# Softmax-weighted values on one core: two heads copied in pairs of row blocks, one check of all values, a skipped loop that counts semaphores in registers

## The chip, the core and the metric

One core of a Trainium2 chip runs the whole program. Its engines are TensorE (PE, with a separate row PEld for weight loads), VectorE (DVE), ScalarE (ACT), GpSimd (POOL) and SyncE (SP); 16 DMA engines move data between DRAM and the on-chip memory SBUF. TensorE writes its results to a second memory, PSUM; the kernel's tiles there take a bank each, 2 KB in each of 128 partitions. The metric is the device time of one execution in microseconds, the median over runs. A profiled execution gives a span, from the first to the last recorded instruction, and its own time, which is a little longer.

## What is computed

```python
def reference(scores, v):            # scores 8 x 12 x 1024 x 1024, v 8 x 12 x 1024 x 64, fp32
    scores_max = np.max(scores, axis=-1, keepdims=True)
    attn = np.exp(scores - scores_max)
    attn = attn / (np.sum(attn, axis=-1, keepdims=True) + 1e-8)
    return np.matmul(attn, v).astype(np.float32)
```

There are 96 heads. For each, the rows of a 1024 x 1024 matrix of scores are turned into weights that sum to one, and these are multiplied with 1024 values of 64 numbers.

## The kernel before

The kernel does not subtract the row maximum. It takes exp(scores) in fp16, appends a column of ones to v, so that one product gives the weighted values and the sum of the weights, and divides. This is right only where sums and values lie in a safe range. The kernel therefore gathers the reciprocal of every row's sum and the largest value of v, tests both, and at the end has a number (`count`) of partitions that passed. If it is less than 128, a second, general loop computes everything again with the maximum subtracted (`general`, line 330); with these inputs it is skipped by a jump (line 469).

The main loop (line 461) runs 24 times over groups of four heads (k = 0 to 3). A head's scores lie as eight row blocks of 128 rows (r = 0 to 7), in one of four buffers `s_nat` of 4 MB. In a head:

- ScalarE takes the exponential of two row blocks at a time (line 414, 128x2048), or of one in the group's last head, into one of eight buffers `p_nat`.
- TensorE turns each block's eight 128x128 pieces (line 427) into a PSUM tile `psT`. There are four, of one block each.
- VectorE copies each `psT` to SBUF, into one of four `pt` (line 434, 128x1024 fp16).
- TensorE multiplies `pt` with `vones`, the values with their ones, eight products into a PSUM bank `psO` (line 173, in `finish`). Four row blocks share a bank, so a head has two banks, and there are two sets. Products follow the turned blocks three row blocks later (`LAG`).
- After the fourth and the eighth block VectorE inverts the sums of the bank into `seen` (`invert`, line 150) and multiplies (`normalise`, line 158, two instructions), into `out_sb`.
- GpSimd converts the values of a head four ahead into `vones` (`spread_v`, line 270, four copies a head).

VectorE also reduces each of the four `vones` to its largest absolute value, twice in head 0 and twice in head 1 (`watch_v`, line 287), and tests these in head 2 (`spread_of`, lines 281 and 282, and `within`, lines 300 and 308). At the group's end `judge` does the same with `seen`, and a product with ones gives `count` (lines 304, 308, 324, 328).

SyncE issues all transfers on one queue, in an order written out by hand (`queue`, `load` at 249, `load_v` at 261, `store` at 194): loads as soon as ScalarE has read a buffer, one store of two heads after head 1 and one after head 3. Each engine's order is a scheduler's, except where `after` or `in_line` fix it: TensorE's whole order, each reduce of `vones` behind a copy, and the last reciprocal of a first bank ahead of the last copy. The main loop lets semaphores count on across iterations and waits against registers (`iteration_sync="reg_based"`); the general loop resets its semaphores in each iteration.

Behind the loop all engines pass a barrier, load `count` into a register (line 468, where SyncE also tests that it lies between 0 and 128), jump over the general loop, and meet in two closing barriers (listed under line 496, the launch). In a barrier each engine reports with a DRAIN and GpSimd releases all.

## Time and profile before

| | |
|---|---|
| median of 3 runs | 1068.48 us (1068.08 to 1069.45) |
| time of the profiled execution | 1067.78 us |
| its span | 1066.0 us |
| mean granted TensorE clock | 0.825 |
| busy: PE, DVE, ACT, POOL | 727.3, 786.2, 741.1, 244.8 us |
| HBM read, written | 436.21 MB, 25.17 MB |

In the profile's groups of instructions a row is a source line with its engine, operation, tiles and count, then its busy time and the mean of one, then the time its engine sat idle before it and what ended that. A row with a small q behind the engine's name is the engine's sequencer (jumps, semaphores, drains, DMA issues), which is not counted as busy. The table by stage gives each engine's busy time in a stretch of the span. Instruction queues in the DMA part carry the engines' own code.

```profile
L434 DVE COPY pt<-psT 128x1024 f16<-128x1024 f16 x768 | 513.9, 687 | 189.1 <-PE L173 77.3
L158 DVE TENSOR_TENSOR out_sb<-psO,seen 64x256 f32<-64x256 f32 x380 | 160.2, 422 | 63.6 <-DMA out_dram<-out_sb 52.4
```

Over the whole span VectorE's largest row is the 768 copies, one for each row block of each head, 687 ns in the mean.

### The profile page before, as it was taken

How to read it: one execution, taken by the hardware profiler on the slowest of the kernel's cores; microseconds unless marked ns; L12 is line 12 of the kernel's file. 1: busy time of each engine (PE TensorE's matmuls, PEld its weight loads, DVE VectorE, ACT ScalarE, POOL GpSimd, SP SyncE). 2: the span in 40 equal slices, each digit the busy share in tenths (PEclk: the TensorE clock that was granted, in tenths of full speed). 3: DMA queues.
4: the chain of work that ended last, by engine and by line, in shares of the span. 5: the costliest groups of instructions: out<-in, count | busy, mean ns of one | idle time of the engine just before them, and what ended most of it. 6: DMA issues, size and time to landing. Idle time of an engine off the chain costs nothing.

```text
span 1066.0 us, 33658 instructions
## 1 busy us (share of the span) xinstructions
PE 727.3 (68%) x12312; PEld 692.9 (65%) x12312; DVE 786.2 (74%) x1660; ACT 741.1 (70%) x484; POOL 244.8 (23%) x406
## 2 busy tenths in 40 slices
PE   2766866677766667676676766767766667666775
PEld 2766756666766667666675766667765667666674
DVE  1876867868678677776777777868677677786786
ACT  3756776666867668586676776666767668586685
POOL 3113212131121311212113211131121311212113
PEclk9888888878788888887888888878788787887888
DMA  9999999999999999999999999999999999999995
GB/s 393 431 423 434 424 438 430 432 432 428 432 433 433 429 436 433 433 433 432 434 427 439 433 433 433 431 435 432 433 432 433 422 440 433 432 432 427 434 427 206
DMA packets 25014, 453.08 MB, mean 425 GB/s; under 512 B 2800, under 2 KB 2800, under 8 KB 9392
## 3 DMA queue, kind: packets, MB, share of 16 engines
q1 hardware_dynamic: 25008, 453.00, 99.1%
q8 instruction: 4, 0.07, 0.0%
q14 instruction: 2, 0.02, 0.0%
HBM read 436.21 MB, written 25.17 MB: 433 GB/s over the span
## 4 chain that ended last, share of the span: by engine, by line
DMA 61%; PE 11%; PEld 8%; ACT 5%; DVE 5%; issue 4%; POOL 2%; SPq 1%; POOLq 1%; ACTq 0%; DVEq 0%
DMA s_nat<-in_scores_dram 61%; PE psT L427 6%; ACT p_nat L414 5%; PE psO L173 5%; PEld L427 5%; DVE pt L434 5%; PEld L173 4%; POOL vones L270 2%; SPq L261 1%; SPq L249 0%; POOLq L270 0%; POOLq L385 0%; POOLq L461 0%; POOLq L389 0%; DVE out_sb L158 0%
## 5 line engine op out<-in xcount | busy, mean ns | idle before, releaser
L414 ACT ACTIVATE p_nat<-s_nat 128x2048 f16<-128x2048 f32 (+1 forms) x456 | 709.4, 1630 | 219.0 <-DMA s_nat<-in_scores_dram 173.2
L427 PE MATMUL psT<-order,p_nat 128*128 128x128 f16 x6144 | 570.3, 251 | 227.5 <-ACT p_nat L414 216.3
L434 DVE COPY pt<-psT 128x1024 f16<-128x1024 f16 x768 | 513.9, 687 | 189.1 <-PE L173 77.3
L427 PEld LDWEIGHTS <-p_nat 128*128 128x128 f16 x6144 | 461.3, 125 | 244.8 <-ACT p_nat L414 232.6
L270 POOL CAST vones<-v_sb 32x512 f16<-32x512 f32 x400 | 244.1, 610 | 814.1 <-PE L427 385.0
L173 PE MATMUL psO<-vones,pt 128*128 128x65 f16 x6144 | 358.5, 205 | 34.6 <-DVE pt L434 33.0
L173 PEld LDWEIGHTS <-pt 128*128 128x128 f16 x6144 | 301.2, 106 | 48.7 <-DVE pt L434 42.6
L158 DVE TENSOR_TENSOR out_sb<-psO,seen 64x256 f32<-64x256 f32 x380 | 160.2, 422 | 63.6 <-DMA out_dram<-out_sb 52.4
L414 ACT ACT_TABLE_LOAD x24 | 30.8, 1283 | 94.1 <-PE psO L173 52.8
L287 DVE TENSOR_REDUCE v_seen<-vones 128x1 f32<-128x512 f16 x96 | 65.1, 679 | 0.8
L324 PE MATMUL psO<-vones,right 128*1 128x1 f16 x24 | 3.9, 164 | 69.2 <-DVE right L308 69.2
L324 PEld LDWEIGHTS <-right 128*1 128x1 f16 x24 | 1.9, 79 | 72.2 <-DVE right L308 72.2
L150 DVE RECIPROCAL seen<-psO 128x4 f32<-128x4 f32 x192 | 33.7, 176 | 8.6 <-PE psO L173 8.6
L308 DVE SCALAR_TENSOR_TENSOR right<-seen,part 128x1 f16<-128x1 f32 x24 | 10.5, 437 | 0.8
L308 DVE SCALAR_TENSOR_TENSOR fits<-v_seen,part 128x1 f32<-128x1 f32 x24 | 10.0, 415 | 0.0
L328 DVE CAST count<-psO 1x1 int32<-1x1 f32 x24 | 3.5, 146 | 6.2 <-PE psO L324 6.2
L304 DVE SCALAR_TENSOR_TENSOR part<-seen,fits 128x1 f32<-128x1 f32 x24 | 4.6, 192 | 0.8
L281 DVE TENSOR_REDUCE seen<-seen 128x1 f32<-128x33 f32 x24 | 4.5, 187 | 0.8
L281 DVE TENSOR_REDUCE v_seen<-v_seen 128x1 f32<-128x5 f32 x24 | 3.8, 159 | 0.7
L282 DVE TENSOR_REDUCE seen<-seen 128x1 f32<-128x33 f32 x24 | 4.2, 177 | 0.0
L282 DVE TENSOR_REDUCE v_seen<-v_seen 128x1 f32<-128x5 f32 x24 | 3.6, 149 | 0.0
L300 DVE TENSOR_SCALAR part<-v_seen 128x1 f32<-128x1 f32 x24 | 3.5, 144 | 0.0
(12 smaller groups left out, 2.8 us busy)
## 6 DMA issues: line engine op xcount, KB each, us to landing
s_nat<-in_scores_dram SPq DMA_DIRECT2D x96, 4096.0 KB, 32.3
v_sb<-in_v_dram SPq DMA_DIRECT2D x24, 1024.0 KB, 18.5
out_dram<-out_sb SPq DMA_DIRECT2D x47, 512.0 KB, 26.2
s_nat<-in_scores_dram SPq DMA_DIRECT2D x2, 2048.0 KB, 31.3
s_nat<-in_scores_dram SPq DMA_DIRECT2D x1, 1536.0 KB, 32.2
s_nat<-in_scores_dram SPq DMA_DIRECT2D x3, 512.0 KB, 20.7
s_nat<-in_scores_dram SPq DMA_DIRECT2D x1, 1024.0 KB, 25.1
out_dram<-out_sb SPq DMA_DIRECT2D x1, 256.0 KB, 3.0
```

The lines of the kernel that those rows point to most:

```text
L150: return nc.vector.reciprocal(out=recip, in_=psO[:, :, D : D + 1])
L158: nc.vector.tensor_tensor(out=st["out_sb"][h * W : (h + 1) * W, t, b * G : (b + 1) * G, :], in0=psO[part, :, 0:D], in1=recip[part].to_broa ...
L173: product = nc.tensor.matmul(out=bank[:, g * M : (g + 1) * M], lhsT=pt[:, c * P : (c + 1) * P], rhs=st["vones"][:, c, 0:M], start=(c == 0) ...
L261: nc.sync.dma_start(out=v_sb[:].rearrange("x h s l d -> x (h s l d)"), in_=rows[bass.ds(n // AHEAD, 1)].rearrange("o x y -> (o x) y"),)
L270: spread = nc.gpsimd.tensor_copy(out=vones_bufs[k][s * Q : (s + 1) * Q, :, 0:D].rearrange("i (h l) d -> i h l d", l=L), in_=v_sb[k * Q : ( ...
L281: nc.vector.tensor_reduce(out=tile[:, 0:1], in_=tile[:, 0 : n + 1], axis=X, op=ALU.min)
L282: nc.vector.tensor_reduce(out=tile[:, n + 1 : n + 2], in_=tile[:, 1 : n + 2], axis=X, op=ALU.max)
L287: watch = nc.vector.tensor_reduce(out=v_seen[:, 1 + k : 2 + k], in_=vones_bufs[k][:, :, 0:D], axis=mybir.AxisListType.XY, op=ALU.max, appl ...
L308: nc.vector.scalar_tensor_tensor(out=out, in0=tile[:, 0:1], scalar=low, in1=part, op0=ALU.is_ge, op1=ALU.mult)
L414: exp = nc.scalar.activation(out=p_nat[:, g : g + rows, :].rearrange("p r (x v) -> p x r v", v=Q * L), in_=s_bufs[k][:, r + g : r + g + ro ...
L427: turned = nc.tensor.transpose(out=psT[:, c * P : (c + 1) * P], in_=p_row[:, c // L, c % L, :], identity=order16[:],)
L434: copy = nc.vector.tensor_copy(out=pt[:], in_=psT[:])
```

## The change

Six things are changed.

1. `psT` and `pt` become two tiles of two row blocks each. In heads 0 and 1 VectorE copies a pair with one instruction of 128x2048; in heads 2 and 3 it copies row block by row block as before.
2. The two `psO` banks of a head become one tile. Head 0 is inverted and normalised once, after its eighth block, with one reciprocal of 128x8 and two multiplications of 64x512; the other heads as before.
3. The four `vones` become one tile. One reduce in head 0, after its sixth row block, finds the largest absolute value of all four heads, and two small instructions test it against both bounds into `fits`, which GpSimd sets to one ahead of the loop.
4. `judge` contains the test of the sums directly.
5. `values_load` no longer tests the range of `count` while running.
6. The general loop counts semaphores in registers, and some of its VectorE work goes to ScalarE and GpSimd. It is still skipped.

```diff
...
-    vones_bufs = []
-    for k in range(AHEAD):
-        vo = const_pool.tile([P, C, D + 2], FP16, name=f"vones{k}")
-        nc.vector.memset(vo[:, :, D : D + 2], 1.0)
...
+    vones = const_pool.tile([P, AHEAD, C, D + 2], FP16, name="vones")
+    nc.vector.memset(vones[:, :, :, D : D + 2], 1.0)
...
-    pt_bufs = buffers(sb_pool, 4, [P, SK], FP16, "pt")
+    pt_bufs = buffers(sb_pool, 2, [P, EB, SK], FP16, "pt")
...
-    psT_bufs = buffers(ps_pool, 4, [P, SK], FP16, "psT")
...
-    psO_bufs = buffers(ps_pool, 2 * (R // G), [P, 512], FP32, "psO")
+    psT_bufs = buffers(ps_pool, 2, [P, EB, SK], FP16, "psT")
...
+    psO_bufs = buffers(ps_pool, 2, [P, R // G, 512], FP32, "psO")
...
-    def sums(k, st, b):
-
-        psO = st["psO"][b][:, 0 : G * M].rearrange("p (g m) -> p g m", m=M)
+    def sums(k, st, *banks):
+
+        b, n = banks[0], len(banks)
+        psO = st["psO"][:, b : b + n, 0 : G * M].rearrange("p b (g m) -> p b g m", m=M)
         at = 1 + k * R + b * G
-        recip = seen[:, at : at + G].rearrange("p (g o) -> p g o", o=1)
+        recip = seen[:, at : at + n * G].rearrange("p (b g o) -> p b g o", b=n, o=1)
         return psO, recip
 
...
+    def invert(k, st, *banks):
+        psO, recip = sums(k, st, *banks)
+        return nc.vector.reciprocal(out=recip, in_=psO[:, :, :, D : D + 1])
+
+    def normalise(k, st, *banks):
+
+        psO, recip = sums(k, st, *banks)
+        b, n, h = banks[0], len(banks), k % T
         for t in range(T):
             part = slice(t * W, (t + 1) * W)
             nc.vector.tensor_tensor(
-                out=st["out_sb"][h * W : (h + 1) * W, t, b * G : (b + 1) * G, :],
-                in0=psO[part, :, 0:D],
-                in1=recip[part].to_broadcast([W, G, D]),
+                out=st["out_sb"][h * W : (h + 1) * W, t, b * G : (b + n) * G, :].rearrange(
+                    "x (b g) d -> x b g d", b=n
+                ),
+                in0=psO[part, :, :, 0:D],
+                in1=recip[part].to_broadcast([W, n, G, D]),
                 op=mybir.AluOpType.mult,
...
-        bank = st["psO"][b]
         for c in range(C):
             product = nc.tensor.matmul(
-                out=bank[:, g * M : (g + 1) * M],
+                out=st["psO"][:, b, g * M : (g + 1) * M],
...
-                rhs=st["vones"][:, c, 0:M],
+                rhs=vones[:, k, c, 0:M],
                 start=(c == 0),
...
-        if g == G - 1 and k < AHEAD - 1:
+        if k == 0 and r == R - 1:
+            invert(k, st, 0, 1)
+            normalise(k, st, 0, 1)
+        if 0 < k < AHEAD - 1 and g == G - 1:
             invert(k, st, b)
             normalise(k, st, b)
...
-    def spread_of(tile, n):
-
-        nc.vector.tensor_reduce(out=tile[:, 0:1], in_=tile[:, 0 : n + 1], axis=X, op=ALU.min)
-        nc.vector.tensor_reduce(
-            out=tile[:, n + 1 : n + 2], in_=tile[:, 1 : n + 2], axis=X, op=ALU.max
-        )
-
-    def watch_v(k, behind):
+    def watch_v(behind):
+
         watch = nc.vector.tensor_reduce(
-            out=v_seen[:, 1 + k : 2 + k],
-            in_=vones_bufs[k][:, :, 0:D],
-            axis=mybir.AxisListType.XY,
+            out=most,
+            in_=vones[:, :, :, 0:D],
+            axis=mybir.AxisListType.XYZ,
             op=ALU.max,
             apply_absolute_value=True,
         )
         after(watch, behind)
         watches.append(watch)
-
-    def within(out, tile, n, low, high, also=None):
-        part = small("part")
-        if also is None:
-            nc.vector.tensor_scalar(
-                out=part, in0=tile[:, n + 1 : n + 2], scalar1=high, scalar2=None, op0=ALU.is_le
-            )
-        else:
+        for bound, op in ((V_MIN, ALU.is_ge), (V_MAX, ALU.is_le)):
             nc.vector.scalar_tensor_tensor(
-                out=part, in0=tile[:, n + 1 : n + 2], scalar=high, in1=also,
-                op0=ALU.is_le, op1=ALU.mult,
-            )
-        nc.vector.scalar_tensor_tensor(
-            out=out, in0=tile[:, 0:1], scalar=low, in1=part, op0=ALU.is_ge, op1=ALU.mult
-        )
+                out=fits, in0=most, scalar=bound, in1=fits, op0=op, op1=ALU.mult
+            )
...
     count = small_pool.tile([1, 1], I32, name="count")
-    fits, right = small("fits"), small("right", FP16)
+    most, fits, right = small("most"), small("fits"), small("right", FP16)
+    nc.gpsimd.memset(fits, 1.0)
 
     def judge(bank):
 
-        within(right, seen, AHEAD * R, 1.0 / SUM_MAX, 1.0, also=fits[:])
-        cell = bank[0:1, G * M : G * M + 1]
+        n = AHEAD * R
+        part = small("part")
+        nc.vector.tensor_reduce(out=seen[:, 0:1], in_=seen[:, 0 : n + 1], axis=X, op=ALU.min)
+        nc.vector.tensor_reduce(
+            out=seen[:, n + 1 : n + 2], in_=seen[:, 1 : n + 2], axis=X, op=ALU.max
+        )
+        nc.vector.scalar_tensor_tensor(
+            out=part, in0=seen[:, n + 1 : n + 2], scalar=1.0, in1=fits, op0=ALU.is_le, op1=ALU.mult
+        )
+        nc.vector.scalar_tensor_tensor(
+            out=right, in0=seen[:, 0:1], scalar=1.0 / SUM_MAX, in1=part, op0=ALU.is_ge, op1=ALU.mult
+        )
+        cell = bank[0:1, 1, G * M : G * M + 1]
         in_line(
             nc.tensor.matmul(
-                out=cell, lhsT=right[:], rhs=vones_bufs[0][:, 0, D : D + 1], start=True, stop=True
...
-        nc.vector.memset(s_bufs[0][:, 3, 0 : C * M], 1.0)
+        nc.gpsimd.memset(s_bufs[0][:, 3, 0 : C * M], 1.0)
         half = SK // 2
-        with tc.For_i(0, BH * R, 1) as n:
+        with tc.For_i(0, BH * R, 1, iteration_sync="reg_based") as n:
...
             for h in range(2):
-                nc.vector.tensor_copy(out=pt[:, h * half : (h + 1) * half], in_=psO_bufs[h][:, 0:half])
+                nc.scalar.copy(out=pt[:, h * half : (h + 1) * half], in_=psO_bufs[0][:, h, 0:half])
...
-            nc.vector.tensor_scalar(
-                out=out_row, in0=psO_bufs[2][:, 0:D], scalar1=den[:], scalar2=None, op0=ALU.mult
-            )
+            nc.scalar.mul(out_row, psO_bufs[1][:, 0, 0:D], den[:])
...
-            st = dict(vones=vones_bufs[k], psO=[take(psO_bufs) for b in range(R // G)])
+            st = dict(psO=take(psO_bufs))
...
-                psT = take(psT_bufs)
+                if r % EB == 0:
+                    psT2, pt2 = take(psT_bufs), take(pt_bufs)
+                psT, pt = psT2[:, r % EB, :], pt2[:, r % EB, :]
                 for c in range(C):
                     turned = nc.tensor.transpose(
                         out=psT[:, c * P : (c + 1) * P],
                         identity=order16[:],
                     )
                     in_line(turned)
-                pt = take(pt_bufs)
-                copy = nc.vector.tensor_copy(out=pt[:], in_=psT[:])
-                rewrite(pt, copy)
-                if k < AHEAD // 2 and r in (G - 1, R - 2):
-                    watch_v(2 * k + (r > G), copy)
-                if k == AHEAD // 2 and r == 1:
-                    spread_of(v_seen, AHEAD)
-                    within(fits, v_seen, AHEAD, V_MIN, V_MAX)
+                if k < 2 and r % EB == EB - 1:
+                    copy = nc.vector.tensor_copy(out=pt2[:], in_=psT2[:])
+                    rewrite(pt2, copy)
+                if k >= 2:
+                    copy = nc.vector.tensor_copy(out=pt, in_=psT)
+                    rewrite(pt2, copy)
+                if k == 0 and r == R - 3:
+                    watch_v(copy)
                 if k == AHEAD - 1 and r == R - 1:
                     after(copy, invert(k, st, 0))
                 if r == R - 1:
...
-        spread_of(seen, AHEAD * R)
-        judge(st["psO"][-1])
+        judge(st["psO"])
...
-    good = nc.values_load(count[:], min_val=0, max_val=P)
+    good = nc.values_load(
+        count[:], min_val=0, max_val=P,
+        skip_runtime_bounds_check_because="a count of partitions, which is compared and no address",
+    )
     with tc.If(good < P, preferred_fallthrough_block=False):
```

More of the change, by code (lines that the diff above doesn't have):

```diff
@@ L215, in end @@
         for g in range(G):
-            nc.scalar.mul(done[:, g * D : (g + 1) * D], psO[:, g, 0:D], recip[:, g, :])
+            nc.scalar.mul(done[:, g * D : (g + 1) * D], psO[:, 0, g, 0:D], recip[:, 0, g, :])
         invert(k, st, 1)
@@ L219, in end @@
         nc.vector.tensor_tensor(
-            out=done[:, G * D :].rearrange("p (g d) -> p g d", d=D),
-            in0=psO[:, :, 0:D],
-            in1=recip.to_broadcast([P, G, D]),
+            out=done[:, G * D :].rearrange("p (b g d) -> p b g d", b=1, d=D),
+            in0=psO[:, :, :, 0:D],
+            in1=recip.to_broadcast([P, 1, G, D]),
             op=ALU.mult,
@@ L270, in spread_v @@
             spread = nc.gpsimd.tensor_copy(
-                out=vones_bufs[k][s * Q : (s + 1) * Q, :, 0:D].rearrange(
+                out=vones[s * Q : (s + 1) * Q, k, :, 0:D].rearrange(
                     "i (h l) d -> i h l d", l=L
@@ L316 @@
     count = small_pool.tile([1, 1], I32, name="count")
-    fits, right = small("fits"), small("right", FP16)
+    most, fits, right = small("most"), small("fits"), small("right", FP16)
+    nc.gpsimd.memset(fits, 1.0)
     def judge(bank):
-        within(right, seen, AHEAD * R, 1.0 / SUM_MAX, 1.0, also=fits[:])
-        cell = bank[0:1, G * M : G * M + 1]
+        n = AHEAD * R
[7 more added lines that the diff above has]
+        )
+        nc.vector.scalar_tensor_tensor(
+            out=right, in0=seen[:, 0:1], scalar=1.0 / SUM_MAX, in1=part, op0=ALU.is_ge, op1=ALU.mult
+        )
+        cell = bank[0:1, 1, G * M : G * M + 1]
         in_line(
             nc.tensor.matmul(
-                out=cell, lhsT=right[:], rhs=vones_bufs[0][:, 0, D : D + 1], start=True, stop=True
+                out=cell, lhsT=right[:], rhs=vones[:, 0, 0, D : D + 1], start=True, stop=True
             )
@@ L350, in general @@
                 nc.tensor.transpose(
-                    out=psO_bufs[c * P // half][:, at : at + P],
+                    out=psO_bufs[0][:, c * P // half, at : at + P],
                     in_=p_row[:, c * P : (c + 1) * P],
```

16 lines of the change are left out of this document (3 added, 13 removed).

## The prediction

> **What bounds the kernel now.** I read the page's first parts, then the stages at the end, because the page says at once where nothing can be won.
>
> ```profile
> span 1066.0 us, 33658 instructions
> ...
> DMA  9999999999999999999999999999999999999995
> ...
> q1 hardware_dynamic: 25008, 453.00, 99.1%
> ```
>
> The DMA engines are full in every slice but the last. 453 MB at some 433 GB/s are 1047 us, and no edit here changes a byte of it. So for the first 1049 us only the stream counts. The view of two whole groups of four heads (43.7 us each, 500 to 587.4 us) agrees: DMA share 1.00 in both, while VectorE is busy for 32.9 and 33.4 of 43.7 us. VectorE has about 10 us to spare per group, and what it saves there is worth nothing. What can count is after the stream, so I cut the end into stages (busy us and count by engine, then clock, DMA share, GB/s):
>
> ```profile
> core 0: us, PE busy (x) PEld busy (x) DVE busy (x) ACT busy (x) POOL busy (x), PEclk, DMA share, GB/s
> 1028.00:1035.00 7.00, 5.90 (x128) 5.66 (x126) 6.62 (x13) 5.92 (x4) 0.00 (x0) 0.99 1.01 431
> 1035.00:1042.00 7.00, 6.35 (x128) 5.71 (x126) 6.75 (x14) 6.97 (x5) 0.84 (x2) 1.00 1.00 426
> 1042.00:1049.00 7.00, 5.74 (x122) 5.33 (x120) 6.81 (x18) 6.13 (x5) 4.04 (x7) 1.00 1.01 420
> 1049.00:1056.00 7.00, 5.92 (x115) 4.99 (x112) 6.46 (x14) 5.14 (x9) 2.44 (x4) 1.00 0.48 163
> 1056.00:1061.00 5.00, 0.27 (x5) 0.08 (x1) 1.58 (x7) 0.09 (x1) 2.46 (x4) 0.78 0.24 52
> 1061.00:1066.00 5.00, 0.00 (x0) 0.00 (x0) 0.00 (x0) 0.00 (x0) 0.00 (x0) 0.50 0.02 7
> ```
>
> Two things stand here. From 1028 to 1056 VectorE is nearly full: in the last group it is the bound beside the stream. And in the last 5 us no engine works at all. VectorE's groups from 1028.6 to 1055.7 (count, busy us, mean ns, idle before):
>
> ```profile
> L434 DVE COPY pt<-psT 128x1024 f16<-128x1024 f16 x29 | 18.8, 681 | 0.7 <-PE L173 0.4
> L158 DVE TENSOR_TENSOR out_sb<-psO,seen 64x256 f32<-64x256 f32 x12 | 5.1, 421 | 0.3
> L287 DVE TENSOR_REDUCE v_seen<-vones 128x1 f32<-128x512 f16 x4 | 2.7, 678 | 0.0
> L150 DVE RECIPROCAL seen<-psO 128x4 f32<-128x4 f32 x7 | 1.2, 174 | 0.0
> ```
>
> It waits for 1 us of 27. The idle end is resolved by lines: L469 is the jump over the general loop, L496 the two closing barriers (duration min/median/max, first and last start):
>
> ```profile
> L469 SPq COMPARE_BRANCH  x2: 46/48/49, 1061.8 to 1062.1; - x2
> ...
> L469 PEldq COMPARE_BRANCH  x2: 82/133/184, 1061.9 to 1062.4; - x2
> L469 DVEq COMPARE_BRANCH  x2: 57/59/61, 1061.9 to 1062.2; - x2
> ```
> ```profile
> L496 SPq DRAIN  x2: 7/7/7, 1063.1 to 1063.2; - x2
> ...
> L496 PEldq DRAIN  x1: 8/8/8, 1062.6 to 1062.6; - x1
> L496 DVEq DRAIN  x1: 42/42/42, 1065.2 to 1065.2; - x1
> L496 POOLq EVENT_SEMAPHORE  x1: 17/17/17, 1065.3 to 1065.3; - x1
> ```
>
> Each engine jumps and reports to the barrier with its DRAIN. PE does so at 1062.6, SyncE at 1063.2. VectorE, whose last work ended at 1058.8, jumps at 1062.15 and drains only at 1065.19: 2.98 us for nothing it could wait for. In that gap lie the only instruction transfers of the stage: 16 KB from 1063.04, 8 KB from 1063.17 (queues 8 and 14; in the DMA view q14 has 2 of them, one more at 1065.8). I read it as a jump into code that was not there yet. GpSimd's answer at 1065.27 and the end at 1066.0 hang on it.
>
> **The jump.** Counted in the built programs, VectorE has 212 instructions before and 163 after; its jump goes from number 177 to 208 before, from 137 to 159 after. SyncE jumps from 127 to 172, PE from 1111 to 1153, both farther, without a stall, so distance is not the cause; a block border between 177 and 208 of VectorE is. The loop (20 to 170) runs 24 times and no instruction transfer falls into the later 23, so all code up to 170 stays in place. The new target lies at 159, below that. I take the stall as gone. Bounds: 0 if the border is elsewhere, the whole 2.98 us if not; I take the whole, and then SyncE or PE is last.
>
> [...]
>
> **SyncE and PE behind it.** SyncE's path from its first branch (1061.8) to its DRAIN (1063.2) loses three semaphore instructions of the skipped branch (0.075 apart: 0.23), the range test of values_load (L468: 191 and 37 ns, 0.32 to the next start) and two of eight closing waits (0.06 each: 0.12). 1063.18 - 0.67 = 1062.5. PE loses one semaphore instruction (0.14): 1062.64 - 0.14 = 1062.5. Barrier at 1062.5, GpSimd 0.08 later at 1062.6 instead of 1065.27: **-2.65 us**. If the stall stays, none of this shows, since VectorE is last anyway.
>
> **VectorE in the last group.** Pitches from the timeline: three copies in a row take 1.89 us, so one follows another after 0.60.
> - Copies of heads 0 and 1: 16 x 0.60 = 9.6 go. A pair copy is not in the trace. The reduce rows give the fixed part (128x5: 0.15), so 1024 elements stream for 0.53; a pair is 2 x 0.53 + 0.15 = 1.21 busy, 1.13 in a row: 8 x 1.13 = 9.0, **-0.5**. Bounds: 1.06 (streaming alone), and 2.26 if it streams as slowly per element as the 128x512 reduce (0.53 per 512). I take 1.13; the same operation's row is nearest.
> - Value check: four reduces (0.60 each, 2.4) and four small ones (0.35) go; one reduce of 2048 (4 x 0.53 + 0.15 - 0.08 = 2.2) and two small ones (0.2) come: **-0.35**.
> - Head 0's two normalisations (0.09 + 2 x 0.45 + 0.05 each: 2.1) become one: 0.22 + 2 x 0.72 = 1.65: **-0.45**.
> - Against it: the first copy waits for two transposed blocks, not one. The blocks come 0.85 apart there (PE clock 0.50 from 1024 to 1028), so it starts at 1026.3 instead of 1025.45, and the next two pairs leave gaps of 0.5 and 0.4; twice later VectorE waits 0.3 for products that a pair copy released late: **+0.85 to +2.3**, I take 1.2.
> - From head 1 on the built order puts the two multiplications right behind the reciprocal; before, a copy stood between. Reciprocal to multiplication is 0.22 instead of 0.09, but the copy then loses its 0.11 gap: **+0.02** each, four times.
>
> Sum -1.3 + 1.3: I take **-0.1**, with +0.9 and -0.9 as ends. The gain is capped: the five last exponentials run from 1048.45 to 1053.30 as the last rows land, the last transposes need 0.7 more, so the last copy can't start before 1054.05; now it starts at 1054.96.
>
> **At nothing.** Pair copies, the late normalisation and the single reduce in the other 23 groups: VectorE has 10 us to spare. Were that gone, loads take 32 us to land while 4 MB need 9.7, so they are issued some 22 us ahead. SyncE's stores wait for VectorE only after heads 1 and 3; head 0's normalisation is still earlier than head 1's. Head 0's PSUM pair is next written by head 2. GpSimd's new memset (0.1) lies ahead of a wait for v of 4.3 us. What general() holds is skipped.
>
> **The sum.** The profiled execution took 1067.78 (span 1066.0, 1.8 around it). 1067.78 - 2.65 - 0.1 = 1065.0. The median of the runs is 1068.48, 0.7 above this execution; on that footing 1068.48 - 2.75 = **1065.7**.
>
> **Rivals.**
> [...]
> 2. Slower: a pair copy, reading two PSUM banks, streams at 1 element where the 1024 copy does two. Then 2.26 instead of 1.13, 8 times, on the full VectorE of the last group: +9.0, of which about 1.5 fills the new gaps. 1065.7 + 7.5 = 1073.2. It decides from about 1.5 us a pair (8 x 0.35 eats the 2.75). Against: type and pattern are the same.
> 3. The last group's savings count in full (0.9) and the transfer at 1065.8 goes too, shortening what lies behind the span (up to 0.5): 1064.4.
>
> **How the numbers follow.** Forecast 0.74, rival 1 0.12, rival 2 0.07, rival 3 0.07. The forecast's own range is 1064.9 to 1066.6 (-0.9 to +0.9 of the last group, mostly inside). With rivals 1 and 3 the range is 1064.4 to 1068.3; rival 2 and the edges are left out. A difference counts from 0.2%, 2.1 us, about what a measurement can tell from no change. Of the forecast 0.64 lies beyond it, 0.10 within (last group 0.6 worse or more). Faster 0.64 + 0.07 = 0.71, same 0.10 + 0.12 = 0.22, slower 0.07.
>
> **What would show it.** In the new profile: VectorE's DRAIN within 0.3 us of its jump; SyncE's or PE's DRAIN last; no 8 KB instruction transfer between jump and barrier. The idle stretch behind the last store shrinks from about 4.5 to 2 us. Pair copies of 1.2 us mean; the last copy within 0.9 us of 1054.96; DMA full to 1049. Wrong would be: a DRAIN 3 us behind its jump on any engine, pair copies beyond 1.5 us, or a slice of the stream below 9.

## The result: slower, and the profile after

The changed kernel takes 1076.22 us (1075.81 to 1077.07), the kernel before in the same runs 1068.28 us: a ratio of 1.0074, with an interval from 1.0061 to 1.0087: 0.7% slower, little but clear of noise. That is 7.9 us more where 2.75 us less was forecast. The profiled execution took 1076.2 us, with a span of 1074.4 us.

The page of the changed kernel first: its span, the DMA engines in 40 slices, and the queues.

```profile
span 1074.4 us, 32373 instructions
...
DMA  9999999999999999999999999999999999999992
...
q1 hardware_dynamic: 25008, 453.00, 98.3%
q8 instruction: 4, 0.07, 0.0%
```

The stream is as full as it was, and it ends almost at the same time: the last exponential ends at 1053.8 us, before at 1053.3. So next to nothing was lost in the loads, and nearly all in what the engines do with the last group. And the queue q14, which had carried two instruction transfers of 8 KB, is gone. The stages of the end, with the columns as before:

```profile
1028.00:1035.00 7.00, 6.91 (x104) 6.75 (x103) 4.21 (x4) 5.92 (x4) 0.00 (x0) 0.69 1.03 437
1035.00:1042.00 7.00, 4.09 (x88) 3.78 (x85) 6.42 (x9) 6.89 (x5) 0.34 (x1) 1.00 0.99 421
1042.00:1049.00 7.00, 4.27 (x88) 4.00 (x89) 5.29 (x9) 6.12 (x5) 2.08 (x4) 1.00 1.01 420
1049.00:1056.00 7.00, 4.41 (x88) 4.12 (x88) 5.81 (x12) 4.84 (x5) 2.42 (x4) 1.00 0.31 128
1056.00:1063.00 7.00, 4.62 (x98) 4.38 (x96) 4.72 (x10) 0.00 (x0) 2.42 (x4) 1.00 0.17 37
1063.00:1070.00 7.00, 2.49 (x54) 2.08 (x52) 3.35 (x11) 0.93 (x4) 2.44 (x4) 0.99 0.01 2
1070.00:1074.40 4.40, 0.00 (x0) 0.00 (x0) 0.09 (x1) 0.00 (x0) 0.00 (x0) 0.50 0.26 60
```

Before, VectorE (third column) was busy for 6.5 to 6.8 of each 7 us and TensorE (first) for about 6. From 1035 to 1063 us TensorE is now busy for 4.1 to 4.6 us and VectorE for 4.7 to 6.4, and the work ends 10 us later. Neither is full there: the two wait for each other. VectorE's groups between the first copy of the last group and the last (1027.2 to 1065.8 us; count, busy us, mean ns, idle before and who ended it) and TensorE's waits from 1024 to 1068 us (us, times, longest) say where:

```profile
L430 DVE COPY pt<-psT 128x1024 f16<-128x1024 f16 x16 | 11.0, 691 | 5.2 <-PE L168 3.5 <-PE psO L168 1.5
L427 DVE COPY pt<-psT 128x2048 f16<-128x2048 f16 x8 | 9.7, 1221 | 3.7 <-PE L420 2.2 <-PE psO L168 1.5
L152 DVE TENSOR_TENSOR out_sb<-psO,seen 64x256 f32<-64x256 f32 x8 | 3.4, 422 | 0.3
L279 DVE TENSOR_REDUCE most<-vones 128x1 f32<-128x2048 f16 x1 | 2.3, 2276 | 0.0
L152 DVE TENSOR_TENSOR out_sb<-psO,seen 64x512 f32<-64x512 f32 x2 | 1.4, 688 | 0.1
```
```profile
PE psT L420 <- DVE pt L430: 6.4, 8, 0.8
...
PE psO L168 <- DVE out_sb L152: 1.6, 2, 1.3
```

TensorE's waits before, from 1024 to 1058 us, have neither:

```profile
PE psO L173 <- DVE pt L434: 2.0, 6, 0.7
PE psT L427 <- ACT p_nat L414: 1.9, 6, 0.9
```

VectorE's instructions cost what the prediction gave them (a pair copy 1.22 us, the one reduce 2.28), but VectorE now waits 5.2 us ahead of its single copies and 3.7 ahead of its pair copies. The wait that the kernel before did not have is TensorE's: eight times, once for each pair of blocks in heads 2 and 3, a transposition waits for the copy `L430`. The timeline of one such pair (start, duration, and in brackets the idle time before) shows the round trip:

```profile
1051.22 0.69 DVE L430 COPY pt<-psT 128x1024 f16<-128x1024 f16 x1
...
1051.96 0.61 PE L420 MATMUL psT<-order,p_nat 128*128 128x128 f16 x8 [0.81 <-DVE pt L430]
...
1052.64 0.69 DVE L430 COPY pt<-psT 128x1024 f16<-128x1024 f16 x1 [0.73 <-PE L168]
1052.66 0.61 PE L420 MATMUL psT<-order,p_nat 128*128 128x128 f16 x8
...
1053.60 0.69 DVE L430 COPY pt<-psT 128x1024 f16<-128x1024 f16 x1 [0.27 <-PE psO L168]
...
1054.34 0.27 PE L420 MATMUL psT<-order,p_nat 128*128 128x128 f16 x2 [0.81 <-DVE pt L430]
```

TensorE turns an even block at 1052.66. VectorE copies it at 1053.60, and only when that copy has ended (1054.29) does TensorE start on the odd block of the same pair, at 1054.34, although that block goes to the other half of the tile. Two blocks take 2.38 us; before, VectorE alone set the pace.

The end of the program did what was forecast. The jump over the general loop (`L464`) and the DRAIN behind it (`L491`), with first and last start:

```profile
L464 DVEq COMPARE_BRANCH  x2: 57/59/61, 1073.1 to 1073.2; - x2
```
```profile
L491 SPq DRAIN  x3: 7/7/7, 1073.7 to 1074.0; - x3
...
L491 DVEq DRAIN  x2: 10/10/10, 1073.4 to 1074.0; - x2
L491 PEldq DRAIN  x2: 8/37/66, 1073.7 to 1074.0; - x2
```

VectorE's DRAIN starts 0.22 us after its last jump starts (1073.23 to 1073.45); before it was 3.04 (1062.15 to 1065.19; the 2.98 of the prediction count from the end of the jump). SyncE is last at 1073.73, as forecast, behind TensorE's DRAIN at 1073.66. From the last reciprocal (1056.88 before, 1068.09 now) to the end of the span it is 9.1 us before and 6.3 now: 2.8 us won. The last copy ends 10.1 us later (1055.6, now 1065.7), and that reciprocal comes 2.4 us behind it instead of 1.3: 10.1 + 1.1 - 2.8 = 8.4 us, the difference of the spans.

Where the 10.1 us of the last copy come from can be read from three marks: the first transposition of the last group (1024.40 before, 1027.37 now), the end of the last copy of its head 1 (1041.18, 1046.53) and that of its head 3 (1055.62, 1065.71). The group starts 3.0 us late, heads 0 and 1 take 2.4 us more, heads 2 and 3 take 4.7 us more. Of the 2.4 us, 0.9 is order alone: two multiplications of head 1 now stand ahead of its last copy (from 1044.40), and stood behind it before (from 1041.21).

### The profile page after: what moved, and what is told of

It is laid out like the page before. It is cut to its first block, busy times and chain, and to the rows that moved or that the text cites. A ratio compares the mean times of both kernels' runs of the same rounds, so it can differ in the third digit from the quotient of the medians.

```text
span 1074.4 us, 32373 instructions
## 1 busy us (share of the span) xinstructions
PE 661.3 (62%) x12312; PEld 620.5 (58%) x12312; DVE 746.5 (69%) x1272; ACT 741.1 (69%) x484; POOL 243.5 (23%) x407
## 4 chain that ended last, share of the span: by engine, by line
PEld 38%; issue 29%; PE 20%; DVE 9%; PEldq 1%; ACT 1%; DVEq 0%; ACTq 0%
PEld L420 24%; PE psT L420 14%; PEld L168 13%; PE psO L168 7%; DVE pt L427 5%; DVE pt L430 2%; ACT p_nat L405 1%; DVE out_sb L152 1%; DVE part L309 0%; DVE fits L289 0%; PEldq L453 0%; DVE right L312 0%; PEldq L376 0%; DVE seen L144 0%; PEldq L380 0%
## 5 line engine op out<-in xcount | busy, mean ns | idle before, releaser
L420 PE MATMUL psT<-order,p_nat 128*128 128x128 f16 x6144 | 507.6, 234 | 180.9 <-DVE pt L430 149.0
L420 PEld LDWEIGHTS <-p_nat 128*128 128x128 f16 x6144 | 429.9, 119 | 198.4 <-issue 172.7
L168 PE MATMUL psO<-vones,pt 128*128 128x65 f16 x6144 | 322.5, 196 | 138.0 <-DVE out_sb L152 51.1
L168 PEld LDWEIGHTS <-pt 128*128 128x128 f16 x6144 | 267.4, 100 | 158.3 <-DVE pt L427 96.0
L430 DVE COPY pt<-psT 128x1024 f16<-128x1024 f16 x384 | 264.0, 691 | 130.9 <-PE L168 78.4
L427 DVE COPY pt<-psT 128x2048 f16<-128x2048 f16 x192 | 232.0, 1221 | 103.5 <-PE L420 82.7
L152 DVE TENSOR_TENSOR out_sb<-psO,seen 64x256 f32<-64x256 f32 (+1 forms) x332 | 152.9, 460 | 50.0 <-PE psO L168 28.3
L279 DVE TENSOR_REDUCE most<-vones 128x1 f32<-128x2048 f16 x24 | 54.6, 2275 | 0.0
L144 DVE RECIPROCAL seen<-psO 128x4 f32<-128x4 f32 (+1 forms) x168 | 30.5, 181 | 29.5 <-PE psT L420 14.8
L214 ACT ACTIVATE done<-psO,seen 128x64 f32<-128x64 f32 x4 | 0.9, 314 | 13.2 <-PE psO L168 13.2
L289 DVE SCALAR_TENSOR_TENSOR fits<-most,fits 128x1 f32<-128x1 f32 x48 | 7.1, 148 | 0.0
```

The costliest lines, as they stand in the source:

```text
L144: return nc.vector.reciprocal(out=recip, in_=psO[:, :, :, D : D + 1])
L152: nc.vector.tensor_tensor(out=st["out_sb"][h * W : (h + 1) * W, t, b * G : (b + n) * G, :].rearrange("x (b g) d -> x b g d", b=n), in0=psO ...
L168: product = nc.tensor.matmul(out=st["psO"][:, b, g * M : (g + 1) * M], lhsT=pt[:, c * P : (c + 1) * P], rhs=vones[:, k, c, 0:M], start=(c ...
L279: watch = nc.vector.tensor_reduce(out=most, in_=vones[:, :, :, 0:D], axis=mybir.AxisListType.XYZ, op=ALU.max, apply_absolute_value=True,)
L289: nc.vector.scalar_tensor_tensor(out=fits, in0=most, scalar=bound, in1=fits, op0=op, op1=ALU.mult)
L420: turned = nc.tensor.transpose(out=psT[:, c * P : (c + 1) * P], in_=p_row[:, c // L, c % L, :], identity=order16[:],)
```

## The experiments

Every ratio is to the kernel before, timed anew with each set of runs (e1 to e4, e5 to e8, e9 to e12); kernels of different sets are compared by their ratios. The theories in the expectations, formed as the runs came in: **A**, the two blocks of a `psT` and a `pt` pair are one tile, and what writes one half waits for what reads the other. **B**, the pair copies themselves are slow, since they wait for two blocks. **C**, VectorE's new instructions (the long reduce, the late normalisation) hold it up. **D**, the two banks of a `psO` pair are tied together in the same way as the halves in A.

### e1 to e4: the pairs of psT and pt

e1 and e2 declare accesses to different halves independent of each other, which takes the wait away and nothing else (`apart` is the kernel's own function for this). In e1:

```diff
                     in_line(turned)
+                    if k >= 2 and r % EB == EB - 1:
+                        apart(turned, copy, "two halves of a pair")
+                        apart(copy, turned, "two halves of a pair")
```

> The changed kernel, in which the transposes into the upper half of a psT pair are declared independent of the copy out of its lower half (heads 2 and 3; the two touch different elements). Theory A: the last group ends 10.1 us late because in heads 2 and 3 a pair is one tile, so TensorE may not turn the odd block before VectorE has copied the even one, and may go on only then; the 2.4 us that two blocks take there (before: about 1.8) are this round trip. By A the copies of heads 2 and 3 lose their 4.8 us, the group before ends earlier as well, so the last group starts up to 2 us sooner, and the time falls from 1076.2 to 1068 to 1071 (the copy of an even block still waits for the products of the other half of its pt pair). Theory B: the pair copies of heads 0 and 1 and the late start are to blame: 1075 to 1076.

Measured: 1072.96 us, ratio 1.0041 (1.0027 to 1.0055). e2 adds the same for products of an odd block and the copy of the next even one into the same `pt` pair (`copies` holds that copy):

```diff
             in_line(product)
+            if r % EB == EB - 1 and copies[-1] is not None:
+                apart(product, copies[-1], "two halves of a pair")
+                apart(copies[-1], product, "two halves of a pair")
...
+                copies.append(copy if k >= 2 and r % EB == 0 else None)
```

> As the run before, and the copy into the lower half of a pt pair is also independent of the products that read its upper half. Theory A: the whole coupling of the two halves is gone, heads 2 and 3 run as in the kernel before; what is left is the later first copy of the group (1.2 by the prediction) and the gain at the jump (2.4): 1066 to 1068. Theory B (pair copies of heads 0 and 1, late start): 1074 to 1076, since nothing of these is changed. Theory C (the one reduce of 2.3 us and the late normalisation of head 0 hold VectorE up): also 1074 to 1076.

Measured: 1073.83 us, 1.0048 (1.0031 to 1.0065). e3 copies pairs in all four heads:

```diff
-                if k < 2 and r % EB == EB - 1:
+                if r % EB == EB - 1:
                     copy = nc.vector.tensor_copy(out=pt2[:], in_=psT2[:])
                     rewrite(pt2, copy)
-                if k >= 2:
-                    copy = nc.vector.tensor_copy(out=pt, in_=psT)
-                    rewrite(pt2, copy)
```

> The changed kernel with pair copies in all four heads, so that no half of a tile is ever copied alone. Theory A: no round trip between the halves is left; heads 2 and 3 cost VectorE less (1.13 a pair), the last pair waits for the last single row (exponential ends at 1053.8, transposes 0.7): last copy from about 1054.8 to 1056, and the time is 1066 to 1069. Theory B: pairs are what is slow (in heads 0 and 1 of the last group 14 blocks take 16 us), so heads 2 and 3 get no better than heads 0 and 1: 1074 or more.

Measured: 1072.51 us, 1.0039 (1.0024 to 1.0053). e4 has no pairs at all:

```diff
-    pt_bufs = buffers(sb_pool, 2, [P, EB, SK], FP16, "pt")
+    pt_bufs = buffers(sb_pool, 4, [P, SK], FP16, "pt")
...
-    psT_bufs = buffers(ps_pool, 2, [P, EB, SK], FP16, "psT")
+    psT_bufs = buffers(ps_pool, 4, [P, SK], FP16, "psT")
...
-                if r % EB == 0:
-                    psT2, pt2 = take(psT_bufs), take(pt_bufs)
-                psT, pt = psT2[:, r % EB, :], pt2[:, r % EB, :]
+                psT = take(psT_bufs)
...
-                if k < 2 and r % EB == EB - 1:
-                    copy = nc.vector.tensor_copy(out=pt2[:], in_=psT2[:])
-                    rewrite(pt2, copy)
-                if k >= 2:
-                    copy = nc.vector.tensor_copy(out=pt, in_=psT)
-                    rewrite(pt2, copy)
+                pt = take(pt_bufs)
+                copy = nc.vector.tensor_copy(out=pt[:], in_=psT[:])
+                rewrite(pt, copy)
```

> The changed kernel without its pairs: psT and pt are four tiles of one block again and every block is copied by itself; the one check of the values, head 0's single normalisation and the shorter programs stay. Theories A and B: everything that was lost hangs on the pairs, so the last copy is back at 1055 to 1056 and the gain at the jump shows: 1065 to 1066.5. Theory C (the reduce of 2.3 us and the late normalisation): 1070 or more.

Measured: 1073.48 us, 1.0048 (1.0031 to 1.0065). All four lie together, some 3 us below the changed kernel and 4 to 5 above the kernel before. All that A expected is missed, though in e1 and e2 no transposition of the last group waits for a single copy any more: that coupling is real, but not all. And e4 speaks against B: without any pair the kernel is as slow as with pairs whose halves are free. e4's time is what C expected; e5 and e8 below rule C out. Something else that all four share costs most of the rest. TensorE's waits of e4 (1024 to 1066 us) and its timeline name it:

```profile
PE psO L168 <- DVE out_sb L152: 6.5, 2, 3.6
```
```profile
1039.80 1.88 DVE L425 COPY pt<-psT 128x1024 f16<-128x1024 f16 x3
...
1041.61 0.17 DVE L144 RECIPROCAL seen<-psO 128x4 f32<-128x4 f32 x1
1041.70 0.66 DVE L425 COPY pt<-psT 128x1024 f16<-128x1024 f16 x1
1042.38 0.88 DVE L152 TENSOR_TENSOR out_sb<-psO,seen 64x256 f32<-64x256 f32 x2
1043.31 0.43 PE L168 MATMUL psO<-vones,pt 128*128 128x65 f16 x8 [3.58 <-DVE out_sb L152]
...
1044.63 0.69 DVE L425 COPY pt<-psT 128x1024 f16<-128x1024 f16 x1 [1.37 <-PE psO L168]
```

TensorE stands still for 3.58 us until VectorE has multiplied out the first bank of the head (`L152`, two instructions from 1042.38). The product that waits writes the second bank. VectorE first works off all that is queued ahead of it, and since TensorE's order is fixed, no transposition passes the waiting product; then VectorE itself runs dry for 1.37 us.

### e5 to e8: the pairs of psO

e5 is e4 with four `psO` tiles of one bank again; head 0 is then inverted and normalised bank by bank:

```diff
-    psO_bufs = buffers(ps_pool, 2, [P, R // G, 512], FP32, "psO")
+    psO_bufs = buffers(ps_pool, 2 * (R // G), [P, 1, 512], FP32, "psO")
...
-        if k == 0 and r == R - 1:
-            invert(k, st, 0, 1)
-            normalise(k, st, 0, 1)
-        if 0 < k < AHEAD - 1 and g == G - 1:
+        if k < AHEAD - 1 and g == G - 1:
...
```

> The kernel of e4 (no pairs) in which psO is four tiles of one bank again, so that head 0 is inverted and normalised bank by bank as in the kernel before. Theory D, formed after e1 to e4: a psO pair is one tile too, so in heads 1 to 3 the first product into its second bank waits until VectorE has read the first bank, and at the end ScalarE's four multiplications of the first bank wait for the last product into the second. By D the two idle times of TensorE in e4 (3.6 and 2.9 us, put down to VectorE's out_sb) go, the last copy is back at 1055 to 1056, and with the stall at the jump gone the time is 1065 to 1066.5. Theory C (the one reduce of 2.3 us holds VectorE up): 1071 to 1073.5, since the reduce stays.

Measured: 1066.26 us, 0.9980 (0.9971 to 0.9990): 0.2% faster than the kernel before, as D expected. e6 makes the same edit on the changed kernel, which keeps its pairs of `psT` and `pt`:

> The changed kernel, pairs and all, with psO as four tiles of one bank again (head 0 inverted and normalised bank by bank). What it costs against e5 is the price of the psT and pt pairs alone. Theory D: the psO part goes (about 5 of the 8 us lost), the round trip between the halves stays in heads 2 and 3 (2.4 us for two blocks in place of 2.1, 8 times) with the late start of the pairs: 1067 to 1070. If the pairs' halves were most of the loss after all: 1072 or more.

Measured: 1074.33 us, 1.0057 (1.0041 to 1.0074). D's 1067 to 1070 is missed: the pairs of `psT` and `pt` alone cost nearly as much as both couplings together, 8 us above e5. Some 1.6 of these belong to the pair copies themselves, as e8 will show. e7 turns it round: the kernel before, with a head's two banks made one tile, and no other edit but to the indices in the general loop, which is skipped:

```diff
-    psO_bufs = buffers(ps_pool, 2 * (R // G), [P, 512], FP32, "psO")
+    psO_bufs = buffers(ps_pool, 2, [P, R // G, 512], FP32, "psO")
...
-                psO=[take(psO_bufs) for b in range(R // G)])
+                psO=pair(take(psO_bufs)))
```

> The kernel before with one edit: the two psO banks of a head are one tile. All instructions of all engines are the same, head 0 is still normalised bank by bank. Theory D: each head's first product into the second bank waits for VectorE, in head 0 too, and the stall at the jump stays: 1074 to 1077. Theory C, or any theory that blames VectorE's instructions: 1068 to 1069, no change.

Measured: 1093.67 us, 1.0238 (1.0220 to 1.0255): 25 us for the shape of one tile, with the same instructions. The direction is D's; the size (1074 to 1077) was missed, for a reason that the table below shows. TensorE's waits from 500 to 587.4 us, nearly two of its groups, name the wait:

```profile
PE psO L176 <- DVE out_sb L161: 19.2, 6, 3.7
```

e8 is e2 with the two banks declared independent in heads 1 to 3. Every instruction of the changed kernel is kept:

```diff
+            if b == 1 and k > 0:
+                upper.setdefault(k, []).append(product)
+                for op in lower.get(k, []):
+                    banks_apart(product, op)
...
-        return nc.vector.reciprocal(out=recip, in_=psO[:, :, :, D : D + 1])
+        op = nc.vector.reciprocal(out=recip, in_=psO[:, :, :, D : D + 1])
+        return reads_lower(k, op) if banks == (0,) else op
...
```

Here `banks_apart` calls `apart` both ways, and `reads_lower` does so for whatever reads the first bank: the reciprocal, the two multiplications, and ScalarE's four at the end.

> The kernel of e2 (the halves of a psT and a pt pair independent) in which products into the second psO bank are declared independent of what reads the first one, in heads 1 to 3. Every instruction of the changed kernel stays, the pair copies, the one reduce and the single normalisation of head 0 too; only waits between different halves go. Theory D: with both couplings gone this is what the prediction priced: 1064.5 to 1066.5. If VectorE's own instructions are to blame: 1070 or more.

Measured: 1067.90 us, 0.9994 (0.9985 to 1.0004). This settles C as the cause of the loss, for VectorE does in it all that it does in the changed kernel. It is also 1.4 us above D's range (1064.5 to 1066.5), and its interval holds 1: free of both couplings the change is even, not faster. TensorE's waits of e8 (1024 to 1068 us) hold neither of the two any more; the round trip shrank from 6.4 to 0.2 us:

```profile
PE psO L171 <- DVE pt L454: 3.0, 3, 1.7
PE psO L171 <- DVE pt L457: 1.5, 5, 0.5
...
PE psT L444 <- DVE pt L457: 0.2, 1, 0.2
```

It stays 1.6 us above e5. What is left is `L454`, the pair copy: products wait up to 1.7 us for it. From 1024 us to the end of head 1's last copy VectorE waits 4.5 us ahead of its copies and reciprocals, and 2.7 in e12 below, which is the same but for the pairs.

### e9 and e10: the jump

e9 is e5 with 15 one-element copies more in the general loop, which never runs:

```diff
             nc.vector.reciprocal(out=den, in_=den)
+            for _ in range(15):
+                nc.vector.tensor_copy(out=lift, in_=den)
```

> The kernel of e5 with 15 more VectorE copies of one element in the body of the skipped general loop (29 instructions with their semaphores; none of them is ever run). VectorE's jump behind the main loop then goes from number 158 to 209, about where the kernel before jumps to (208), instead of 180. Theory: the 3 us that VectorE needed behind that jump are a fetch of code beyond a block border between 180 and 207. Then the 8 KB instruction transfer between jump and DRAIN is back, VectorE's DRAIN comes 2.5 to 3 us behind its jump, and the time is 1068 to 1069 against e5's 1066.3. Rival: the stall hung on something else that the change removed (the range test of values_load, the reset of the general loop's semaphores): DRAIN 0.2 us behind the jump, 1066 to 1066.5.

Measured: 1068.60 us, 0.9997 (0.9987 to 1.0006); by the ratios 1.8 us above e5. VectorE's jump (`L458`) and DRAIN (`L485`) in e9:

```profile
L458 DVEq COMPARE_BRANCH  x2: 57/59/61, 1063.3 to 1063.4; - x2
```
```profile
L485 DVEq DRAIN  x1: 41/41/41, 1066.3 to 1066.3; - x1
```

The stall is back, 2.9 us from jump to DRAIN, and with it an 8 KB instruction transfer at 1064.41. Instructions that are never run cost it. e10 is the kernel before with points 5 and 6 alone, all of general() as in the changed kernel:

```diff
...
-        with tc.For_i(0, BH * R, 1) as n:
+        with tc.For_i(0, BH * R, 1, iteration_sync="reg_based") as n:
...
-    good = nc.values_load(count[:], min_val=0, max_val=P)
+    good = nc.values_load(
+        count[:], min_val=0, max_val=P,
+        skip_runtime_bounds_check_because="a count of partitions, which is compared and no address",
+    )
```

> The kernel before with points 5 and 6 of the change alone: no range test of count, and the general loop as in the changed kernel. VectorE's work and its main loop are those of before; its jump goes from 176 to 198 instead of 208. If the border lies between 198 and 207, the stall is gone and SyncE's shorter path shows: 1065.5 to 1066.3. If it lies between 180 and 198, the stall stays and covers what SyncE saves: 1068 to 1068.5. Either way it places the border.

Measured: 1067.78 us, 0.9995 (0.9985 to 1.0004). VectorE's DRAIN in e10:

```profile
L497 DVEq DRAIN  x1: 42/42/42, 1065.3 to 1065.3; - x1
```

Its jump was at 1062.4: the stall is there with a target of 198. It is absent with 159 (the changed kernel), 175 (e12) and 180 (e5), and there with 198 (e10), 208 (before) and 209 (e9). The border lies above 180, at or below 198, and neither the range test nor the way the general loop counts has to do with it: e9 has both edits and stalls.

### e11 and e12: one more coupling alone, and the version that is left

e11 is the kernel before with `psT` and `pt` as pairs, every block still copied by itself:

```diff
...
-                psT = take(psT_bufs)
+                if r % EB == 0:
+                    psT2, pt2 = take(psT_bufs), take(pt_bufs)
+                psT, pt = psT2[:, r % EB, :], pt2[:, r % EB, :]
...
```

> The kernel before with one edit: psT and pt are tiles of two blocks each; every block is still copied by itself, with the same instructions on all engines. Theory D: the round trip between the two halves now holds in all four heads (2.4 us for two blocks, normalising included, 16 times, is 38 us against about 30 now), the last copy ends 8 to 13 us later and the stall at the jump stays: 1076 to 1083. If waits between halves are no matter without pair copies: 1068 to 1069.

Measured: 1131.92 us, 1.0589 (1.0571 to 1.0607). Same sign as expected, but 50 us more. TensorE's waits over two of its groups (500 to 592.8 us) show the round trip 32 times, once for each of 2 x 16 pairs:

```profile
PE psT L429 <- DVE pt L435: 28.1, 32, 1.5
```

e12 is e4 with the two banks of a `psO` pair independent, as in e8. Against e5 it has head 0's single normalisation:

> The kernel of e4 (single psT and pt tiles, psO in pairs, head 0 normalised once) with the products into a second psO bank declared independent of what reads the first, in heads 1 to 3. Against e5 it differs by head 0's single normalisation alone (0.45 less VectorE time by the prediction): 1065.5 to 1066.5, the same as e5 or up to 0.5 faster. If the late normalisation of head 0 costs something by itself: 1067 or more.

Measured: 1065.40 us, 0.9969 (0.9958 to 0.9980), the lowest of all, just below what was expected. It cannot be told from e5 by its time; in its trace the last copy ends at 1055.9, in e5 at 1056.3.

### All of them side by side

"Length" is the time from the end of the last group's first copy to the end of its last, in the traces. In the first three rows the last copy ends 2.3 to 2.9 us behind the last exponential (1053.3 to 1053.4), so the arrival of the last rows bounds it as well. e9 and e10, which concern the end alone, are left out.

| kernel | psT, pt | psO | ratio | length, us | last copy ends |
|---|---|---|---|---|---|
| before | single | single | 1 | 29.5 | 1055.6 |
| e12 | single | pair, free | 0.9969 | 29.8 | 1055.9 |
| e5 | single | single | 0.9980 | 29.9 | 1056.3 |
| e8 | pairs, free | pair, free | 0.9994 | 30.1 | 1057.9 |
| e3 | pairs, copied whole in 4 heads | pair, tied | 1.0039 | 32.9 | 1062.9 |
| e1 | pairs, only psT free | pair, tied | 1.0041 | 33.3 | 1063.0 |
| e2 | pairs, free | pair, tied | 1.0048 | 34.4 | 1063.5 |
| e4 | single | pair, tied | 1.0048 | 35.0 | 1063.0 |
| e6 | pairs, tied in heads 2, 3 | single | 1.0057 | 35.3 | 1064.8 |
| after | pairs, tied in heads 2, 3 | pair, tied | 1.0074 | 35.2 | 1065.7 |
| e7 | single | pair, tied in 4 heads | 1.0238 | 37.8 | 1080.5 |
| e11 | pairs, tied in 4 heads | single | 1.0589 | 40.7 | 1120.1 |

Two things are read from it. The couplings do not add: either one stretches the last group from 30 to between 33 and 35 us, both together to 35.2, since TensorE waits out the one while it waits for the other (in the changed kernel only 1.6 us are left of e4's 6.5). And there is a cliff. From one group's first copy to the next one's it is 43.7 us (mean of 20 groups) in every kernel of the table but two, for so long the loads of a group take (a 24th of 453 MB at the 432 GB/s of 500 to 587.4 us in the kernel before); a stretched chain is hidden behind them in all groups but the last. In e7 that period is 44.4 us and in e11 46.0: there the round trips no longer fit, and every group is late by the difference, and 23 periods lie ahead of the last group: 23 x 0.7 = 16 and 23 x 2.3 = 53 us. The last groups of e7 and e11 do start 16.6 and 53.3 us later than before. My expectations for the two had counted the last group only.

## Why the prediction was wrong

**Right in part: what bounds the kernel.** The stream fills all slices but the last, and the groups ahead of the last are hidden behind it, as long as one takes no more than 43.7 us. But "for the first 1049 us only the stream counts" is too strong: the last group's own work starts at 1024 us, and the 3.0 us of its late start arose well before 1049.

**Right: the jump.** The stall is gone and SyncE is last; its path from the first branch to the DRAIN fell from 1.38 to 0.73 us (forecast: 0.67 less). e5, e9 and e10 show it as a matter of where VectorE's jump lands. An 8 KB instruction transfer lies between jump and DRAIN in the kernel before (1063.17 us) and in e9 (1064.41), and the changed kernel's queues show none of 8 KB. That the stall waits for code, and that a block of code ends at the border, is the author's reading: no row of a trace names either, and the runs show only that targets up to 180 go without the stall, and that with those from 198 on the DRAIN comes 2.9 to 3.0 us behind the jump. The upper end of the forecast's range, 1068.3, is an estimate for a stall that stays, 0.2 us below the median of before. No run singles out these 0.2 us: in the changed kernel the stall is gone, and where it stays with points 5 and 6 alone (e10) the ratio is 0.9995, with 1 inside its interval.

**Right: the price of VectorE's instructions.** A pair copy is 1.22 us (forecast 1.21), the one reduce 2.28 (its working gave 2.27), the two long multiplications 0.69 each (0.72). Rival 2, a pair copy at half speed, is out. With single copies, the rest of VectorE's new work leaves the last group even: e12's last copy ends 0.3 us later than before.

**Wrong: the step "Against it".** It priced two things, that a pair copy waits for two blocks, and that VectorE waits twice for products, at 0.85 to 2.3 us together, and took 1.2; less the 0.5 that the pair copies save, that is 0.7. Freed of the couplings, the pairs do make VectorE wait about that much longer (4.5 us in e8, 2.7 in e12), but the net is more than 0.7: e8's last copy ends 2.0 us behind e12's. So this term was mis-sized, by some 1.3 us, and the pairs take up most of the gain at the jump: e8's ratio is 0.9994, e12's 0.9969. But the step also asked only what VectorE waits for, and only in heads 0 and 1, where it copies pairs. In heads 2 and 3 the same tiles are used by halves, and there TensorE waits for VectorE. From the end of head 1's last copy to the last copy of all it is 19.18 us, and 14.44 before (1046.53 to 1065.71, 1041.18 to 1055.62): 4.7 us.

**Wrong: the step "At nothing".** It said that head 0's `psO` pair is next written by head 2, and so that the merged tile costs nothing. True for head 0, and not looked at in heads 1 to 3, whose first bank is still read while the second is written. e4 against e12 gives the price of this coupling alone: 1.0048 against 0.9969, some 8 us. At the very end it also holds ScalarE: its four multiplications of the first bank wait until the last product into the second, and the last reciprocal waits for them. The waits of the changed kernel from 1024 to 1070 us (the 13.2 us count from ScalarE's last exponential; what costs is that they end only with the last product):

```profile
ACT done L214 <- PE psO L168: 13.2, 1, 13.2
...
DVE seen L144 <- ACT done L214: 2.4, 1, 2.4
```

**Its consequence.** The group before ends later too (last copy at 1022.5, before 1020.4), so the last group starts late: its first transposition comes at 1027.4 us, before at 1024.4. The prediction had the start where it was, but for the wait of the first pair.

**The two parts of the miss.** The result lies 10.5 us above the forecast of 1065.7. The changed kernel against e8 (1.0074 against 0.9994) puts 8.5 us of it to the couplings; the other 2 are still there in e8, which keeps the pairs. That the pairs' price makes up all of these 2 us is not shown.

The sign, then, did not come from the cost that was mis-sized, which leaves the change even, but from one that was not in the list. The change was read for what its instructions do, and the two edits that only make tiles larger were taken for notation. It had a rival that ends slower, at 1073.2 us, with the wrong mechanism; that it comes within 3 us of the result is luck. And none of the three signs that the prediction named for being wrong came (a DRAIN 3 us behind its jump, pair copies beyond 1.5 us, a slice of the stream below 9): all three asked after single instructions or the stream, none after a wait between engines. Of the signs for being right, the place of the last copy failed: it starts at 1065.0 us, not within 0.9 us of 1054.96. The profile of before could have led there: VectorE waits 1 us of 27 in the last group, so TensorE nearly always has the next block ready, and that lead is just what a tile that both share takes away.

## What to carry to other kernels

A tile is also the unit in which accesses wait for each other here (in e11 the shape of two tiles alone makes TensorE wait 32 times in 92.8 us, for 28.1 us): before merging two, list for each use what writes one half while the other is read, on every engine and in every branch of the loop, and check in the built program which instructions gained a wait. If one instruction needs both halves and others use them singly, declare the halves independent, as e12 does; it is what turned +0.74% into -0.31% together with giving up the pair copies. And a chain that has slack in each loop round has it up to a point: compare its whole length with the period, for in these runs the last round paid in full, and beyond the period of 43.7 us every round did (e7 with 44.4 us lost 25 us in all, e11 with 46.0 lost 63).

## What the runs showed of the hardware that was not expected

- Code that is never run cost time here. With 29 more unused VectorE instructions between a jump and its target, e9 takes 1.8 us more than e5 by the ratios, and VectorE's DRAIN comes 2.9 us behind its jump; in the changed kernel, with a target of 159, it is 0.22.
- Longer waits of TensorE for VectorE did not always go with a higher granted TensorE clock. Its mean is 0.825 before; in three kernels in which TensorE has waits for VectorE that the kernel before does not have it is 0.928 (the changed kernel, 6.4 us in the last group), 0.910 (e11, 28.1 us in two groups) and 0.820 (e4, 6.5 us in the last group). What sets it was not tested. With 12312 matmuls in both, TensorE's busy time fell from 727.3 us before to 661.3 in the changed kernel, so the profile's busy row looks better in the slower kernel.
- One VectorE copy of 128x2048 that reads two banks of PSUM takes 1221 ns (the changed kernel's 192), two of 128x1024 take 2 x 687 = 1374 (the 768 of the kernel before): no price of the second bank shows, and the one copy is 0.15 us shorter than the two.
